# VectorE in emission order in the projection part of a Conformer layer, with new estimates in the emission's planner

## The chip, the cores and the metric

The kernel runs on one core of a Trainium2 chip. The metric is device time in microseconds (us) of one execution, as the median of several runs. PE is TensorE's matmul row in the profile, PEld its weight loads, DVE is VectorE, ACT ScalarE, POOL GpSimd, and SP the queue that issues most transfers.

## The reference, cut to what matters

One layer of a streaming encoder is computed in float32 for a prompt of 2048 frames and a sample of 64 frames with cached keys, values and convolution rows. D is 1024.

```python
h = rms_norm(x, norm1_g) * (1 + sc1) + sh1          # modulation: silu(c) @ w_ada + b_ada
glu_a, glu_b, q, k, v, g_conv, g_attn = split(h @ w_in)
u = glu_a * sigmoid(glu_b)
y = silu(layer_norm(causal_depthwise_conv(u, w_dw, 31 taps) + b_dw)); conv_out = y @ w_conv_out
q, k = rms_norm per head (8 heads of 64)
p = softmax(q k^T / 8 + rel_bias[clipped distance], own chunk of 64 and 8 chunks before)
attn_out = (p v) @ w_attn_out
x = x + gt1 * ((sigmoid(g_conv) * conv_out + sigmoid(g_attn) * attn_out) @ w_o)
h2 = rms_norm(x, norm2_g) * (1 + sc2) + sh2
x = x + gt2 * ((silu(gate) * up) @ w_ffn_out)       # gate, up = split(h2 @ w_ffn_in)
```

Outputs are the new rows of prompt and sample, and the states of convolution, keys and values.

## The kernel before, in words

**Precision.** A float32 operand is split into a high part, rounded by an ACT copy, and a low part, the DVE or POOL difference (`split`, L681). A product is three matmuls: high by high, high by low, low by high (`mm3`, L675). So nearly every result on its way to the next product passes ACT, then DVE.

**Two parts.** The first, the projection part, goes over four token blocks of 576 or 512 tokens (`PBLOCKS`). In each block the stages come in the order q, 0, k, 1, v, 2, 3, g (`ORDER`): the projections q, k and v (`qkv`, L1100); four stages 0 to 3 of the gated convolution input, 128 channels each (`glu`, L1141); and the two gates g (`gates`, L1244). Beside those matmuls run the attention heads of the block before or of the same block (`attend`, L1380), the convolution (`convolve`, L1167), its layer norm (`conv_norm`, L1186), and the norm and transposes of the next block's tokens (`norm_tile`, L1076). Attention goes over eight heads per block, and in block 0 eight heads of the sample besides: 40 heads. The second part merges the branches and does the output projection and the feed-forward layer over three token blocks. In the profile it begins at about 1222 us.

**Work on DVE in the projection part.** A convolution stage is 31 instructions per 128 channels over 512 or 606 columns, the taps: one `tensor_scalar`, then 30 `scalar_tensor_tensor` into tile y. They need nothing but u and the tap before. Beside them stand short links in chains of other engines: per score tile, the mask-and-maximum (`softmax_max`, L1279: tile pr, with the maximum in sm), then an exponential on ACT, then a reciprocal and a scaling on DVE (`softmax_scale`, L1294); the low halves pl of the transposed weights; the norms of q and k (kn, ssq); the low halves part_l of what is stored (`store_kq` L950, `conv_norm`, `finish_head` L1322), whose high halves part_h come from ACT. part_h and part_l have two buffers each (NS, L732), which a store to device memory empties. DVE also copies results out of PSUM (u, vst, h) and splits weights at their first use (wlo).

**What sets the order.** The Python code emits instructions in one sequence and keeps a planner beside it. `Meter` (L84) wraps each engine; every emission passes `Stream.add` (L176), which adds an estimated duration to that engine's estimated clock (`load`). L101, the line of the wrapper, is therefore the line of nearly all instructions in the profile, and they are told apart by tiles. PE's estimated clock is the planner's "now". Every 500 estimated ns (STEP_NS) a tick calls the lanes (`Lane`, L106): norm_lane, work, attn, tail and conv. A lane lets its next generator emit a step when the step's due time has come and the engines' estimated backlogs over PE are under the lane's room: 2000 ns of DVE for conv (CONV_ROOM), up to four taps per tick; 3000 ns of DVE and 4000 ns of ACT for attn. A step names when it may go on, as the estimated end of an engine's work (`when`, L197) plus a lag: PE_LAG is 400 ns, DMA_LAG, the allowance for a transfer, 4000 ns. `softmax_max` is called directly behind the score matmuls, in the same step; the taps come from the conv lane in later pumps. At the start of a block's stage 0, `conv.drain()` (L1540) emits what is left of the taps.

The order on the chip is not yet that of emission. When the program is built, the framework's scheduler puts each engine's instructions in order by its own model: among those that its model holds ready, it takes the one emitted first. An instruction whose inputs it holds not ready is passed by later ones. Semaphores follow from that order. Each engine then works through its list.

Of the kernel before, what the change touches and what calls it, by code (L numbers as in the profile page):

```python
# [63 lines left out]
def token_tiles(lo, hi):  # L64
    head = [(0, SMP)] if lo == 0 else []
    return head + [(t, P) for t in range(max(lo, SMP), hi, P)]
# [39 lines left out]
class Lane:  # L106
# [7 lines left out]
    def add(self, gen):  # L114
        self.gens.append([gen, 0.0, {}])
# [52 lines left out]
class Stream:  # L168
# [7 lines left out]
    def add(self, name, op, n, args, kw):  # L176
        if name == "pe":
            x = args[1]
            if op == "transpose":
                ns = 128 / 1.2  # L180
            elif x.dtype == F32:
                ns = max(n, 64) / (2.4 if "tile_position" in kw else 0.6)
            else:
                ns = (n if n >= 256 else 512) / 2.4
        elif name == "act":
            ns = 220 + 0.83 * n
        elif name == "pool":
            ns = 260.0 * n if ALU.pow in args else 60 + 2.25 * n
        else:
            fast = op in ("tensor_scalar", "tensor_copy")  # L190
            ns = 75 + n * (8.3 if op == "reciprocal" else 0.75 if fast else 1.04)
        self.load[name] = max(self.load[name], self.load["pe"]) + ns

    def full(self, room):
# [392 lines left out]
def streaming_layer(ctx: ExitStack, tc: tile.TileContext, I, O):  # L587
# [87 lines left out]
    def mm3(ps, lh, ll, rh, rl, first, last, **kw):  # L675
        pe.matmul(ps, lh, rh, start=first, stop=False, **kw)
        pe.matmul(ps, lh, rl, start=False, stop=False, **kw)
        pe.matmul(ps, ll, rh, start=False, stop=last, **kw)
        stream.spend()

    def split(hi, lo, src):  # L681
        act.activation(hi, src, AF.Copy)
        stream.after("dve", "act")
        dve.tensor_tensor(lo, src, hi.bitcast(F32), ALU.subtract)
# [49 lines left out]
    def temp(name, shape=(P, 512)):  # L734
        return wk.tile(list(shape), F32, tag="t", name=name, bufs=NT)
# [62 lines left out]
    def mod_sums(pa, keys):  # L798


        for i, key in enumerate(keys):
            w = M.get(key)
            a, b = w.shape[1:]
            for j in range(4):

                k, c = divmod(j * 2 * P, b)
                pe.matmul(
                    pa[32 * j : 32 * j + 32], cl[:, a * i + k], w[:, k, c : c + 2 * P], start=i == 0,
                    stop=i == len(keys) - 1, tile_position=(0, 32 * j),
                )  # L810
            M.done()

    def mod_rows(pa):
        R = temp("R", pa.shape)
        stream.after("dve", "pe")
        dve.tensor_copy(R, pa)
        return R

    def mod_columns(pc, R, c6, ct, nh):


        pc = pc.rearrange("p (e n) -> p e n", e=2)
        for e in range(2):
            pe.matmul(pc[:, e], R[:, e * P : e * P + P], sel, start=True, stop=True)
        stream.after("dve", "pe")
        pc = pc[:, :, 2 * (nh - 1) : 2 * (2 * nh - 1)].rearrange("p e (h s) -> p e h s", h=nh)
        cs = slice(ct, ct + 2 * nh)

        def place(a):
            return a[:, cs].rearrange("p (h e) s -> p e h s", e=2)  # L830

        def wide(a):
            return a.rearrange("p (h e) -> p e h", e=2).unsqueeze(3).to_broadcast([P, 2, nh, 2])

        bias = wide(b_ada[:, 8 * c6 + ct : 8 * c6 + ct + 2 * nh])
        gates_of = lambda i: gates_c[:, i].rearrange("p s k -> p k s")
        out = place({0: B1, 1: A1, 3: B2, 4: A2}[c6] if c6 not in (2, 5) else gates_of((2, 5).index(c6)))
        dve.tensor_tensor(out, pc, bias, ALU.add)
        if c6 in (1, 4):
            dve.tensor_tensor(out, out, wide({1: g1, 4: g2}[c6][:, cs]), ALU.mult)  # L840
        elif c6 in (2, 5):
            dve.tensor_scalar(out, out, {2: 0.25, 5: 0.5}[c6], None, ALU.mult)
# [22 lines left out]
    def first_block(xs):  # L865

        tiles = token_tiles(*PBLOCKS[0])
        vectors, taps = setup()
        taps = taps()
        for x_t, (t, n) in zip(xs, tiles):  # L870
            r = square(x_t, n)
            dve.tensor_scalar(x_t[:n], x_t[:n], r, None, ALU.mult)

        def modulation(ct):

            pa = ps_a.tile([P, 512], F32, tag="o", name="pa")
            cs = [slice(c6 * 2 * P, (c6 + 1) * 2 * P) for c6 in range(2)]
            for c6, c in enumerate(cs):
                mod_sums(pa[:, c], [("mod", c6, ct // 2, h, 0) for h in range(2)])
            R = mod_rows(pa)  # L880

            def rest():
                for c6, c in enumerate(cs):
                    mod_columns(pa[:, c], R[:, c], c6, ct, 1)

            return rest

        def turn(k):
            pt = ps_a.tile([P, 2, 512], F32, tag="s", name="pt")
            for i, (t, n) in enumerate(tiles):  # L890
                o = pt[:, 0, t : t + n] if i < 4 else pt[:, 1, :n]
                pe.transpose(o, xs[i][:n, k * P : (k + 1) * P], ident[:n, :n])
            h = wk.tile([P, QB + SMP], F32, tag="pr", name="h32", bufs=8)
            for a, e, o, w in ((0, SMP, pt[:, 0, :SMP], 1), (SMP, 448, pt[:, 0, SMP:448], 0), (448, 576, pt[:, 1, :P], 0)):
                dve.tensor_scalar(h[:, a:e], o, A1[:, k, w : w + 1], B1[:, k, w : w + 1], ALU.mult, ALU.add)
            split(hh[:, k], hl[:, k], h)

        rest = modulation(0)
        vectors()
        rest()  # L900
        W.open("", "wst")
        turn(0)
        pss = [ps_g.tile([P, 512], F32, tag="gp", name="ps") for _ in tiles]
        ws = {}

        def product(i, k):
            t, n = tiles[i]
            if k // 2 not in ws:
                ws[k // 2] = W.get(("qkv", 0, k // 2))
            wh, wl = ws[k // 2]  # L910
            mm3(pss[i][:n], hh[:, k, t : t + n], hl[:, k, t : t + n], wh[:, k % 2], wl[:, k % 2], k == 0, k == KT - 1)
            if i == len(tiles) - 1 and k % 2:
                W.done()

        for k in range(KT - 2):
            if k == 2:
                next(taps)
            turn(k + 1)
            if k and k % 2 == 0:
                rest = modulation(k + 2)  # L920
            for i in range(len(tiles)):
                if i == 2 and not k:
                    rest = modulation(k + 2)
                if i == (2 if k else 4) and k % 2 == 0:
                    rest()
                product(i, k)
        turn(KT - 1)
        for i, (t, n) in enumerate(tiles):
            for k in (KT - 2, KT - 1):
                product(i, k)  # L930
            work.start(qk_rows(pss[i], n, gqk[:, 0:1], q_d, t, None, i > 2))
        next(taps, None)
# [82 lines left out]
    def cached_kv():  # L1015
        rows_ = [(src, j) for j in range(CACHE // P) for src in (ck, cv)]
        ts = []
        for i, (src, j) in enumerate(rows_):
            for src_, j_ in rows_[len(ts) : i + 2]:
                t = temp("cache")  # L1020
                nc.sync.dma_start(t, src_[j_ * P : (j_ + 1) * P])
                ts.append((t, stream.load["pe"] + CACHE_LAG))
            t, landed = ts[i]
            yield landed
            if src is ck:
                store_kq(t, P, k_d, j * P)
            else:
                store_v(t, P, j * P)
            yield
# [38 lines left out]
    def square(x_t, n):  # L1068
        ssq = wk.tile([P, 2], F32, tag="ssq", name="ssq", bufs=3)
        for j in range(2):  # L1070
            act.activation(temp("junk")[:n], x_t[:n, 512 * j : 512 * j + 512], AF.Square, accum_out=ssq[:n, j : j + 1])
        stream.after("dve", "act")
        dve.tensor_tensor(ssq[:n, 0:1], ssq[:n, 0:1], ssq[:n, 1:2], ALU.add)
        return rsqrt_mean(wk, ssq[:n, 0:1], n, 1, D)
# [418 lines left out]
    M.fill()  # L1493
    W = Weights((nc.sync, act, dve, gps), wpool, dram, stream, list(weight_order()), source, 3, 5, lambda key: key[0] in KEPT)
    first_block(xs)
    norm_lane.add(cached_kv())
    mods = mod_steps()
    norms = {}
# [55 lines left out]
    conv.drain()  # L1554
    tail.drain()
    stream.flush()
    side.close()
    p1.close()

# [524 lines left out]
```

## Time and profile before

| what | us |
|---|---|
| median of 3 runs | 3047.5 |
| lowest, highest | 3043.02, 3049.83 |
| the profiled execution, its own time | 3036.07 |
| its span, first to last instruction | 3034.3 |
| busy in the span: PE | 2931.0 |
| DVE | 1928.2 |
| ACT | 1263.8 |
| POOL | 1204.7 |

The profiled execution's time is 1.77 us more than its span. Rows of a timeline give the start, the duration, engine, line, operation, out<-in tiles and shapes, and in brackets the engine's idle time before it with what ended it. Rows of waits give who waited for whom: total us, times, longest us. Rows of groups give busy us, mean ns of one, and idle us before. Rows of windows give the busy us of the engines PE, PEld, DVE, ACT and POOL, the granted PE clock as a share of full speed, the share of busy DMA engines, and GB/s. Rows of transfers end in the KB of one and the median us from issue to landing.

### The profile page before, as it was taken

The page shows a single profiled execution, that of the slowest core. Times are in us where ns is not written, and L with a number is a line of the kernel's source. Part 1 is how long each engine was busy: PE and PEld are TensorE (multiplying, and loading weights), DVE is VectorE, ACT ScalarE, POOL GpSimd, SP SyncE. Part 2 cuts the span into 40 slices and gives each one's busy share as a digit, 9 for nine tenths or more (in the row PEclk, how much of TensorE's full clock was granted, in tenths as well). Part 3 has the DMA queues.
Part 4 walks back from the last instruction along what each step waited for, and adds up shares of the span by engine and source line. Part 5 has one row for each costly group of instructions (what it writes and reads, how often), then busy time and mean ns, then how long its engine had stood idle before and what let it go on. Part 6 is the DMA issues. An engine that isn't in the chain of part 4 may idle for free.

```text
span 3034.3 us, 44863 instructions
## 1 busy us (share of the span) xinstructions
PE 2931.0 (97%) x16277; PEld 2603.6 (86%) x16277; DVE 1928.2 (64%) x3668; ACT 1263.8 (42%) x2290; POOL 1204.7 (40%) x785
## 2 busy tenths in 40 slices
PE   7999898999999999989999989999999999999999
PEld 4789776887888788878999889899999998999998
DVE  4897687777977895464444535555665655366565
ACT  2334532452255257464444324534444254344441
POOL 0201110111011102378888633347766343367761
PEclk9999999999999999999999999999999999999999
DMA  9788789888997788886444686433334965333334
GB/s 314 269 297 302 232 290 303 265 266 272 292 294 232 257 264 264 261 284 215 150 143 145 230 298 211 160 115 111 115 94 143 335 220 191 111 95 114 118 92 162
DMA packets 472107, 646.93 MB, mean 213 GB/s; under 512 B 36820, under 2 KB 315208, under 8 KB 471885
## 3 DMA queue, kind: packets, MB, share of 16 engines
q1 hardware_dynamic: 459605, 626.68, 63.1%
q10 hardware_dynamic: 12280, 17.39, 1.6%
q8 instruction: 128, 2.10, 0.3%
q14 instruction: 94, 0.77, 0.1%
HBM read 487.02 MB, written 156.93 MB: 212 GB/s over the span
## 4 chain that ended last, share of the span: by engine, by line
PE 80%; DVE 9%; DMA 4%; ACT 2%; POOL 2%; issue 2%; SPq 1%; ACTq 0%; POOLq 0%; DVEq 0%
PE ps L101 51%; PE pd L101 16%; PE pw L101 6%; DVE y L101 4%; PE po L101 2%; PE sc L101 2%; PE ptp L101 2%; POOL wlo L101 1%; PE pt L101 1%; DVE pr L101 1%; PE pa L101 1%; ACT whi L101 1%; DVE wlo L101 1%; DMA x_t<-in_x_prompt 1%; POOL ws L101 0%
## 5 line engine op out<-in xcount | busy, mean ns | idle before, releaser
L101 POOL TENSOR_TENSOR wlo<-wst,whi 128x1024 fp32r<-128x1024 f32 (+1 forms) x215 | 456.6, 2133 | 343.1 <-ACT whi L101 320.9
L101 PE MATMUL ps<-t,whi 128*128 128x384 f32 (+1 forms) x2112 | 501.8, 322 | 7.2 <-DVE v L101 4.4
L101 ACT ACTIVATE whi<-wst 128x1024 fp32r<-128x1024 f32 (+1 forms) x270 | 261.6, 973 | 339.1 <-PE ps L101 120.7
L101 PE MATMUL ps<-b,whi 128*128 128x384 f32 (+1 forms) x1584 | 380.1, 326 | 8.8 <-ACT early L101 8.4
L101 PEld LDWEIGHTS ps<-t,whi 128*128 128x128 f32 x2112 | 367.8, 188 | 12.9 <-DVE v L101 3.4
L101 DVE SCALAR_TENSOR_TENSOR y<-u,wd,y 128x512 f32<-128x512 f32 (+1 forms) x480 | 369.1, 772 | 6.6
L101 PE MATMUL ps<-hh,whi 128*128 128x512 f32 (+2 forms) x992 | 361.9, 365 | 0.2 <-DVE part_l L101 0.2
L101 PE MATMUL ps<-hh,wlo 128*128 128x512 f32 (+2 forms) x992 | 345.4, 348 | 1.2 <-DMA wlo<-w_din_l 1.2
L101 PE MATMUL ps<-hl,whi 128*128 128x512 f32 (+2 forms) x992 | 345.3, 348 | 0.0
L101 PE MATMUL ps<-t,wlo 128*128 128x384 f32 (+1 forms) x1056 | 339.5, 322 | 4.0 <-POOL wlo L101 4.0
L101 PE MATMUL pd<-whi,hid 128*128 128x512 f32 (+1 forms) x1076 | 342.1, 390 | 1.1 <-ACT hid L101 1.1
L101 DVE TENSOR_TENSOR acc<-acc,pd 128x512 f32<-128x512 f32 (+1 forms) x398 | 269.8, 686 | 95.5 <-PE pd L101 93.4
L101 PEld LDWEIGHTS ps<-b,whi 128*128 128x128 f32 x1584 | 277.9, 189 | 14.5 <-ACT early L101 10.4
L101 PE MATMUL ps<-b,wlo 128*128 128x384 f32 (+1 forms) x792 | 256.3, 324 | 0.0
L101 POOL TENSOR_TENSOR r<-t,mhalf 128x8 f32<-128x8 f32 (+3 forms) x68 | 83.2, 1226 | 392.7 <-DVE t L101 377.7
L101 PEld LDWEIGHTS pd<-whi,hid 128*128 128x128 f32 (+1 forms) x1076 | 197.2, 183 | 47.3 <-ACT hid L101 1.5
L101 POOL TENSOR_TENSOR wlo<-ws,whi 128x512 fp32r<-128x512 f32 x144 | 190.3, 1336 | 80.2 <-ACT whi L101 78.4
L101 POOL TENSOR_TENSOR wlo<-wup,whi 128x1024 fp32r<-128x1024 f32 (+1 forms) x70 | 150.7, 2154 | 150.5 <-ACT whi L101 98.5
L101 PE MATMUL pd<-wlo,hid 128*128 128x512 f32 (+1 forms) x538 | 210.0, 390 | 0.0
L101 PEld LDWEIGHTS ps<-hh,wlo 128*128 128x128 f32 x992 | 187.1, 189 | 23.8 <-DMA wlo<-w_din_l 1.6
L101 PEld LDWEIGHTS ps<-hh,whi 128*128 128x128 f32 x992 | 187.6, 189 | 18.6 <-issue 2.1
L101 PEld LDWEIGHTS ps<-t,wlo 128*128 128x128 f32 x1056 | 198.5, 188 | 5.2 <-POOL wlo L101 4.6
(222 smaller groups left out, 6017.3 us busy)
## 6 DMA issues: line engine op xcount, KB each, us to landing
whi<-w_din_h SPq DMA_DIRECT2D x72, 512.0 KB, 6.1
wlo<-w_din_l SPq DMA_DIRECT2D x72, 512.0 KB, 6.8
wst<-sum_d SPq DMA_DIRECT2D x132, 256.0 KB, 3.0
wfo<-in_w_ffn_out SPq DMA_DIRECT2D x49, 512.0 KB, 5.5
wmod<-in_w_ada SPq DMA_DIRECT2D x48, 512.0 KB, 7.0
sum_d<-ws SPq DMA_DIRECT2D x88, 256.0 KB, 2.0
wst<-in_w_ffn_in SPq DMA_DIRECT2D x84, 256.0 KB, 3.2
wst<-in_w_ffn_in SPq DMA_DIRECT2D x37, 512.0 KB, 5.5
```

The costliest lines, as they stand in the source:

```text
L101: return f(*args, **kw)
```

## The change

Three lines of the planner and a region. In `Stream.add`, a float32r matmul is estimated 13.5 ns longer; a DVE instruction has a fixed part of 240 ns when it is a `scalar_tensor_tensor` (the taps among them) and 110 ns otherwise, where it had 75 ns. These estimates serve the whole kernel. And from behind `first_block` to behind the flush that ends the projection part, a region tells the framework's scheduler to keep DVE's instructions in the order of emission. The other engines, and the transfers' issue order, stay with the scheduler.

```diff
             else:
-                ns = (n if n >= 256 else 512) / 2.4
+                ns = 13.5 + (n if n >= 256 else 512) / 2.4
...
             fast = op in ("tensor_scalar", "tensor_copy")
-            ns = 75 + n * (8.3 if op == "reciprocal" else 0.75 if fast else 1.04)
+            ns = (240 if op == "scalar_tensor_tensor" else 110) + n * (8.3 if op == "reciprocal" else 0.75 if fast else 1.04)
...
     first_block(xs)
+    in_order = tc.manual_schedule(engines={mybir.EngineType.DVE})
+    in_order.__enter__()
     norm_lane.add(cached_kv())
...
     stream.flush()
+    in_order.__exit__(None, None, None)
     side.close()
```

## The prediction

> **What bounds the kernel now.** The page comes first: its span, and the share of the matrix engine PE.
>
> ```profile
> span 3034.3 us, 44863 instructions
> PE 2931.0 (97%) x16277; PEld 2603.6 (86%) x16277; DVE 1928.2 (64%) x3668; ACT 1263.8 (42%) x2290; POOL 1204.7 (40%) x785
> ```
>
> PE is the bound: 103 us of the span are left without it. Next, the table by stage: the projection part's crowded first block, its other blocks, and the rest (columns: PE, PEld, DVE, ACT, POOL busy, clock, DMA share, GB/s).
>
> ```profile
> 100.00:500.00 400.00, 370.41 (x2220) 321.00 (x2219) 318.38 (x662) 149.14 (x325) 49.85 (x51) 0.96 0.83 277
> 500.00:1222.00 722.00, 709.17 (x3846) 594.84 (x3845) 570.31 (x1183) 324.43 (x599) 89.05 (x74) 1.00 0.84 270
> 1222.00:3034.30 1812.30, 1773.23 (x9754) 1634.37 (x9752) 987.31 (x1704) 757.46 (x1308) 1051.61 (x637) 0.99 0.52 171
> ```
>
> In the region of the new order PE lacks 29.6 us in the first 400 and 12.8 us in the next 722, so 42 us are all that an order on DVE could win in idle time. DVE, the VectorE, is busy 80% and 79% there: not the bound, but without much slack. Next, PE's waits in that part (us in total, times, longest).
>
> ```profile
> PE ptp L101 <- DVE pr L101: 14.9, 10, 8.9
> PE sc L101 <- DVE sm L101: 4.4, 7, 1.3
> PE ps L101 <- ACT hh L101: 3.6, 2, 2.9
> PE ps L101 <- DMA whi<-w_dqkv_h: 3.2, 1, 3.2
> ```
>
> The two largest entries are the softmax of the attention heads, made by DVE. One of those waits is the largest stall, 8.9 us; so the timeline around it, DVE first and PE behind.
>
> ```profile
> 463.96 0.75 DVE L101 SCALAR_TENSOR_TENSOR y<-u,wd,y 128x512 f32<-128x512 f32 x1
> ...
> 470.36 4.68 DVE L101 SCALAR_TENSOR_TENSOR y<-u,wd,y 128x512 f32<-128x512 f32 x6
> 474.96 0.48 DVE L101 CUSTOM_DVE_ANT_0 pr<-sc,bias 64x320 f32<-64x320 f32 x1
> ...
> 477.62 0.37 DVE L101 TENSOR_SCALAR pr<-pr,sm 64x320 f32<-64x320 f32 x1
> ```
>
> ```profile
> 468.83 0.46 PE L101 MATMUL sc<-kk,q 128*64 128x320 f32 x2
> 478.14 0.55 PE L101 MATMUL ptp<-ident,pr 64*128 64x64 f32 x3 [8.86 <-DVE pr L101]
> ```
>
> The scores are there at 469.3, yet DVE first works through six convolution taps (y) and takes the scores at 474.96. Nothing else fed PE: it stood until 478.14. By the code softmax_max is emitted straight behind its score matmuls, and the taps that a later tick hands out come behind it. This is the pattern that emission order forbids. It recurs on a smaller scale, around 198 us and at 508 us:
>
> ```profile
> 195.70 2.61 DVE L101 SCALAR_TENSOR_TENSOR y<-u,wd,y 128x606 f32<-128x606 f32 x3
> 198.23 0.28 DVE L101 CUSTOM_DVE_ANT_0 pr<-sc,bias 128x128 f32<-128x128 f32 x1
> ```
>
> ```profile
> 196.02 0.34 PE L101 MATMUL sc<-kk,q 128*128 128x128 f32 x2
> 198.57 0.50 PE L101 MATMUL sc<-kk,q 128*128 128x256 f32 x2 [0.56 <-DVE sm L101]
> 199.74 0.61 PE L101 MATMUL sc<-kk,q 128*128 128x384 f32 x2 [0.67 <-DVE sm L101]
> 201.10 0.79 PE L101 MATMUL sc<-kk,q 128*128 128x512 f32 x2 [0.75 <-DVE sm L101]
> ```
>
> ```profile
> 508.37 0.85 PE L101 MATMUL sc<-kk,q 128*128 128x320 f32 x4 [1.34 <-DVE sm L101]
> ```
>
> **The change, part by part.** The first part, *order*: it removes no work, and adds none. Where it helps, the taps ahead of a softmax go behind it. The stalls shown sum to 8.86 + 0.56 + 0.67 + 0.75 + 1.34 = 12.2 us. I count them as gone; what is late next is the rest of the same softmax chain, on ACT, and projection matmuls run beside that. The clock follows the stalls:
>
> ```profile
> 200.00:210.00 10.00, 8.15 (x38) 7.11 (x38) 8.43 (x23) 4.09 (x10) 0.00 (x0) 0.66 0.99 363
> 480.00:490.00 10.00, 10.00 (x44) 8.25 (x43) 1.14 (x3) 1.07 (x3) 0.00 (x0) 0.92 0.74 239
> ```
>
> In the ten microseconds from 200 a third of the clock was withheld, in those from 480 a twelfth: (1 - 0.66) x 8.15 + (1 - 0.92) x 10.0 = 3.6 us of matmul time. Removal so far: 12.2 + 3.6 = 15.8 us. [...]
>
> Second, *estimates*. A tap of 512 columns was put at 75 + 1.04 x 512 = 607 ns and is now put at 240 + 532 = 772; a matmul of 512 columns goes from 213 to 227, one of 384 from 160 to 173.5.
>
> ```profile
> L101 DVE SCALAR_TENSOR_TENSOR y<-u,wd,y 128x512 f32<-128x512 f32 x360 | 268.3, 748 | 4.7
> ...
> L101 DVE SCALAR_TENSOR_TENSOR y<-u,wd,y 128x512 f32<-128x512 f32 (+1 forms) x480 | 369.1, 772 | 6.6
> ...
> 1954.44 16.36 PE pd L101 x72
> 1970.81 20.82 PE ps L101 x120
> ```
>
> The trace has 748 ns for the tap (six start 0.78 us apart at 470.36), 16.36 / 72 = 227 ns for 512 columns and 20.82 / 120 = 173.5 ns for 384. So the new figures are right, and the old ones let the emission believe that the 480 taps cost about 480 x 0.165 = 79 us less than they do. With an order that is obeyed this matters: a lane hands out taps only while DVE's estimated backlog is under 2.0 us (CONV_ROOM), and PE's consumers are put 0.4 us (PE_LAG) behind DVE's estimated end. I expect the backlog ahead of a softmax to shrink from the six taps above to two or three. I give this no gain of its own; without it the order's gain would not hold.
>
> Third, *what the order costs*. The new wait is at the head of DVE's queue: an instruction that is not ready holds all that stands behind it, the taps and also the copies that free PSUM. Two kinds stand out. The low halves (part_l) wait for ACT's high halves, which wait until a store has emptied one of two buffers; the store's landing is in no estimate. ACT's waits, from 100 to 500 us and then from 500 to 1222:
>
> ```profile
> ACT part_h L101 <- DMA q_d<-part_h: 8.3, 2, 6.0
> ACT part_h L101 <- DMA c_d<-part_h: 3.9, 2, 2.3
> ```
>
> ```profile
> ACT part_h L101 <- DMA k_d<-part_h: 16.2, 2, 8.6
> ACT part_h L101 <- DMA c_d<-part_h: 3.9, 1, 3.9
> ```
>
> ```profile
> DVE part_l L101 <- ACT part_h L101: 9.9, 11, 2.9
> DVE pr L101 <- PE sc L101: 29.6, 31, 3.3
> ```
>
> That is 32.3 us in seven waits, of which DVE shows only 9.9 today, because taps slip past. At 198 us DVE was 198.23 - 196.36 = 1.9 us late and PE lost 0.56, so PE has a lead of about 1.3 to 2 us; I take 2. The seven waits were 6.0, 2.3, 2.3, 1.6, 8.6, 7.6 and 3.9 us, the longest given, its partner the remainder; less 2 each they are 4.0 + 0.3 + 0.3 + 0 + 6.6 + 5.6 + 1.9 = 18.7 us. That is the upper end; the lower end is nothing, because the scheduler still orders PE and can put other matmuls there. I take 4: the 6.0 us wait, in the block where DVE is busy 80% and PE already stalls. Later PE lacks only 12.8 us of 722, though the waits for k_d lie there too, and has projection matmuls to go on with; I cost those at nothing. If that cover is gone, the other waits cost 14.7.
>
> The other kind is the softmax of a new head, whose matmuls wait for loads. The planner counts 4.0 us for a landing; the issues say 5.4 and 5.0:
>
> ```profile
> q<-q_d SPq DMA_DIRECT2D x64, 256.0 KB, 5.4
> kk<-k_d SPq DMA_DIRECT2D x48, 256.0 KB, 5.0
> ```
>
> So DVE may stand 1.4 us at each of 40 heads (8 in each of four blocks, and 8 of the sample), 56 us in all. It has 400 - 318 + 722 - 570 = 234 us idle to put that in, and 1.4 is under PE's lead: nothing for PE. If the lead is only the planned 0.4 us, they cost PE 40 x 1.0 = 40 us.
>
> Fourth, *after 1222 us* only the estimates act. No time of an instruction changes, PE lacks 39 us of 1812, and events tied to PE's estimated clock come 6 to 8% earlier, counted in matmuls. I take nothing, with 6 us to either side.
>
> **Sum.** -15.8 + 4 = about -12 us. The profiled execution took 3036.07 us, 1.8 around its span; it would take 3024. The median of the three timed runs is 3047.5, 0.4% above the profiled one. The prediction is for such a median: 3047.5 - 12 = 3035.5 us.
>
> **The rivals.**
>
> *The queue's head decides* (slower). The same order that stops taps from slipping past also stops them where nothing was lost. Place: part_l and the first softmax of a head. Price: the whole 18.7 us, with the gain cancelled because the late scores at 468.83 now hold DVE from 463.96 on and all later softmaxes shift. 3047.5 + 18.7 = 3066; with the 40 us of the heads, 3106. It decides once a hold exceeds PE's lead of 2 us. For it: seven such waits, and a DVE busy 80%. Against: the largest of these waits lie where PE today loses least. [...]
>
> *More than the named stalls goes.* The two DVE rows of PE's waits are 14.9 + 4.4 = 19.3 us, and the clock of 0.96 in the first stage withholds 0.04 x 370 = 14.8; with 4 us of holds that is -30, or 3017. Against: some of these waits have other causes than taps, and the clock also follows waits for DMA.
>
> *Taps come too late.* Taps at 772 ns fill the 2.0 us sooner, so fewer are handed out per tick and the rest is emitted in one run where a block drains its convolution. Ten taps left in each of three blocks would hold DVE 10 x 0.78 = 7.8 us, less 2 of lead: 17 us, 3065. Against: 80% busy leaves room for all of them.
>
> *It does not change the time.* The scheduler reorders PE, ACT and the DMA queues around the new DVE order, and other stalls replace these: 3047.5, give or take 6.
>
> **How the numbers follow.** A measurement of this kernel can tell about 0.2%, 6 us, from no change. Forecast (6 to 22 us faster) 0.32; more than that 0.12; no change 0.14; the queue's head 0.30; late taps 0.12. So faster 0.44, same 0.14, slower 0.42. The forecast's own range is 3025 to 3041. Both signs hold much of the chance, so the range for 8 in 10 goes from 3010, past the large gain, to 3085, half of the heads' 40 us on top of 3066.
>
> **What would show it.** Right: no run of taps between the end of a score matmul and its softmax; PE's wait for pr under 5 us in total; PE busy above 375 of 400 us in the first stage; clock above 0.96 there. Wrong: DVE's idle time rises above 300 us, with part_l and pr waiting longest, and PE waits for copies out of PSUM (u, vst, kn), or PE lacks more than 45 us after 1222.

## The result, and the profile after

The changed kernel takes 3087.05 us (median of 4 runs, 3085.94 to 3088.94), the kernel before, run beside it, 3046.13 us (median of 4, 3043.02 to 3049.83): a ratio of 1.0143, 95% interval 1.0126 to 1.0161. It is **slower** by 41 us. The prediction said 3035.5, and its range ended at 3085. The profiled execution of the changed kernel took 3085.94 us.

The page of the changed kernel: its span, the busy time of the engines, and the chain of work that ended last by engine.

```profile
span 3084.1 us, 44919 instructions
...
PE 2954.7 (96%) x16277; PEld 2611.6 (85%) x16277; DVE 1945.5 (63%) x3668; ACT 1262.5 (41%) x2290; POOL 1208.0 (39%) x785
...
PE 73%; DVE 10%; DMA 9%; ACT 3%; issue 2%; POOL 2%; SPq 1%; ACTq 0%; DVEq 0%; POOLq 0%
```

The work is the same (16277 matmuls, 3668 DVE instructions), but transfers are 9% of the chain, against 4% on the page of before. The stages, as they were shown of before:

```profile
100.00:500.00 400.00, 370.08 (x2213) 318.85 (x2215) 323.32 (x665) 149.23 (x325) 51.72 (x49) 0.97 0.84 276
500.00:1222.00 722.00, 692.28 (x3654) 567.84 (x3642) 560.46 (x1135) 288.97 (x546) 72.02 (x68) 0.98 0.80 259
1222.00:3084.10 1862.10, 1816.28 (x9957) 1672.02 (x9957) 1013.90 (x1758) 791.04 (x1362) 1070.52 (x647) 0.99 0.52 171
```

The first 400 us hold 2213 matmuls where they held 2220: nothing won, nothing lost. The next 722 us hold 3654 instead of 3846. At 709.17 / 3846 = 0.184 us each, those 192 missing matmuls are 35 us. That is where most of the time goes. The first matmul of the next stage (tile cin) shows the whole loss of the projection part; of before, then of after, shortest, median and longest ns, and first and last start:

```profile
L101 PE MATMUL ps<-cin,whi x768: 277/334/687, 1219.9 to 2500.1; 128*128 128x384 f32 x128, 128*128 128x320 f32 x32, 128*128 128x256 f32 x32
```

```profile
L101 PE MATMUL ps<-cin,whi x768: 274/334/657, 1264.4 to 2548.3; 128*128 128x384 f32 x128, 128*128 128x320 f32 x32, 128*128 128x256 f32 x32
```

It starts 44.5 us later; the spans differ by 49.8, so some 5 us more are lost behind it, and nearly all of the loss is inside the region of the new order. Next, what VectorE waits for from 100 to 1260 us (total us, times, longest), before and then after:

```profile
DVE pr L101 <- PE sc L101: 30.9, 32, 3.3
DVE part_l L101 <- ACT part_h L101: 10.9, 13, 2.9
DVE pr L101 <- DMA bias<-rb_d: 2.2, 3, 1.1
```

```profile
DVE pr L101 <- PE sc L101: 93.1, 35, 9.6
DVE pr L101 <- DMA bias<-rb_d: 30.5, 6, 7.1
...
DVE part_l L101 <- ACT part_h L101: 16.4, 13, 4.8
```

The two waits of a softmax (pr), for its scores and for its bias, went from 33.1 to 123.6 us; part_l hardly moved. One such wait, close up: VectorE, then PE, then SP's issues, and the ten microseconds from 1160.

```profile
1157.26 0.75 DVE L101 SCALAR_TENSOR_TENSOR y<-u,wd,y 128x512 f32<-128x512 f32 x1
1163.60 0.82 DVE L101 CUSTOM_DVE_ANT_0 pr<-sc,bias 128x640 f32<-128x640 f32 x1 [5.59 <-DMA bias<-rb_d]
```

```profile
1151.86 0.74 PE L101 MATMUL sc<-kk,q 128*128 128x320 f32 x4
...
1159.73 0.50 PE L101 MATMUL po<-ph,vv 128*128 128x512 f32 x1
1162.19 0.82 PE L101 MATMUL sc<-kk,q 128*128 128x320 f32 x4 [1.96 <-DMA kk<-k_d]
1164.49 1.43 PE L101 MATMUL sc<-kk,q 128*128 128x320 f32 x4 [1.48 <-DVE sm L101]
```

```profile
1152.63 0.60 SPq L1308 DMA_DIRECT2D q<-q_d  x1
...
1155.32 1.94 SPq L1352 DMA_DIRECT2D bias<-rb_d  x2
```

```profile
1160.00:1170.00 10.00, 5.75 (x18) 4.41 (x18) 6.30 (x14) 3.28 (x7) 0.00 (x0) 0.66 0.41 111
```

The new head's first transfer is issued at 1152.63; the last of its six is issued until 1157.26, and VectorE gets the bias at 1163.6, about 11 us after the first issue. The planner counts 4.0 us for this. The loads could not be issued sooner: by the code q and kk have one buffer each (`load_qk`, bufs=1), and the last scores that read them ended at 1151.86 + 0.74 = 1152.60. VectorE's next instruction in emission order is that softmax, so it stands for 5.59 us and the taps stay behind it. PE ends its other work, waits 1.96 us for kk and 1.48 for the softmax, and a third of its clock is withheld: in these ten microseconds it is busy 5.75 us. The clock in the trace is half from 1163.16 to 1169.98. A stretch ahead of that, then its two halves:

```profile
1159.75:1163.16 3.41, 1.30 (x7) 0.75 (x5) 0.00 (x0) 0.91 (x2) 0.00 (x0) 1.00 1.02 242
1163.16:1166.57 3.41, 1.43 (x4) 1.03 (x4) 2.90 (x6) 0.93 (x2) 0.00 (x0) 0.50 0.25 97
1166.57:1169.98 3.41, 3.25 (x9) 2.77 (x10) 3.38 (x8) 1.68 (x3) 0.00 (x0) 0.50 0.00 0
```

In the first of them PE was busy 1.30 us at the full clock; in the next two the clock was half, also in the last, where PE was busy 3.25 us. In the stretch ahead of the half clock PE's longest gap was 1.96 us, and PE was busy 38% of it.

PE's waits for kk itself, from 100 us to the end of that part, before and then after:

```profile
PE sc L101 <- DMA kk<-k_d: 1.8, 2, 1.2
```

```profile
PE sc L101 <- DMA kk<-k_d: 10.2, 9, 2.0
```

So the late loads reach PE by two ways: through VectorE, and at the head of PE's own queue.

### The profile page after: what moved, and what is told of

Its sections match the earlier page's. It is cut to its first block, busy times and chain, and to the rows that moved or that the text cites. A ratio compares the mean times of both kernels' runs of the same rounds, so it can differ in the third digit from the quotient of the medians.

```text
span 3084.1 us, 44919 instructions
## 1 busy us (share of the span) xinstructions
PE 2954.7 (96%) x16277; PEld 2611.6 (85%) x16277; DVE 1945.5 (63%) x3668; ACT 1262.5 (41%) x2290; POOL 1208.0 (39%) x785
## 4 chain that ended last, share of the span: by engine, by line
PE 73%; DVE 10%; DMA 9%; ACT 3%; issue 2%; POOL 2%; SPq 1%; ACTq 0%; DVEq 0%; POOLq 0%
PE ps L101 45%; PE pd L101 15%; PE pw L101 6%; DVE y L101 5%; PE sc L101 2%; PE po L101 2%; DMA kk<-k_d 2%; PE ptp L101 1%; DVE pr L101 1%; DMA bias<-rb_d 1%; POOL wlo L101 1%; PE pt L101 1%; DVE pl L101 1%; DVE wlo L101 1%; PE pa L101 1%
## 5 line engine op out<-in xcount | busy, mean ns | idle before, releaser
L101 DVE TENSOR_TENSOR acc<-acc,pd 128x512 f32<-128x512 f32 (+1 forms) x398 | 269.9, 686 | 95.3 <-PE pd L101 93.3
L101 PEld LDWEIGHTS pd<-whi,hid 128*128 128x128 f32 (+1 forms) x1076 | 197.2, 183 | 45.8
L101 PEld LDWEIGHTS ps<-hh,whi 128*128 128x128 f32 x992 | 188.2, 190 | 23.8 <-ACT gate L101 4.3
L101 PE MATMUL ps<-cin,whi 128*128 128x384 f32 (+2 forms) x768 | 188.6, 332 | 16.4 <-DVE t L101 9.9
```

Of the source, the lines that this page charges most:

```text
L101: return f(*args, **kw)
```

## The experiments

Theory **H**: in emission order a head's first softmax stands at VectorE's queue head until q, kk and bias have landed, and the allowance of 4.0 us in `fetch` puts it there too early. Rival **T**: the new estimates hand out taps or attention too late. Rival **P**: part_l behind the stores. Each run is compared with runs of the kernel before on the same chip (medians 3040.4 to 3043.3 in four groups), by ratio.

**The order alone.** The region, with the old estimates.

```diff
+    in_order = tc.manual_schedule(engines={mybir.EngineType.DVE})
+    in_order.__enter__()
...
+    in_order.__exit__(None, None, None)
```

> The region of emission order, with the old estimates. Theory H (the head of VectorE's queue stands for a new head's loads, whose landing the planner puts at 4.0 us): the order alone is the cause, so at least as slow as the change, 3075 to 3110 us, with VectorE's waits for sc and bias near 120 us. Rival T (the new estimates make taps and attention late): the order alone is near the kernel before, 3040 to 3055.

3088.53 us, ratio 1.015 [1.0134, 1.0166]: the whole loss. Its VectorE waits from 100 to 1260 are 93.3 us for scores and bias, under the 120 foretold, and 44.1 for part_l:

```profile
DVE pr L101 <- PE sc L101: 83.0, 45, 12.9
DVE part_l L101 <- ACT part_h L101: 44.1, 18, 6.5
DVE pr L101 <- DMA bias<-rb_d: 10.3, 3, 5.4
```

**The estimates alone.** The two lines of `Stream.add`, without the region.

> The new estimates without the region. Theory H: within 10 us of the kernel before, 3036 to 3056 us. Rival T: most of the loss is here, 3070 to 3090, with VectorE's waits for sc and bias near the 32 us of before.

3046.62 us, ratio 1.0017 [1.0007, 1.0027]: T falls as the cause of the 41 us. The estimates cost at most 0.3% by themselves.

**A longer allowance.** The change, with 8.0 us in `fetch` only.

```diff
-            loaded[i] = stream.load["pe"] + DMA_LAG
+            loaded[i] = stream.load["pe"] + HEAD_LAG   # 8000.0
```

> The change, with the planner's allowance for the loads of a new head raised from 4.0 to 8.0 us (that one place, other allowances as they were). Theory H: VectorE's waits for sc and bias fall from 124 us to under 60, and the time to 3045 to 3065 us. Rival T and rival P (part_l behind the stores that empty its two buffers): 3080 to 3095, since neither is touched.

3036.71 us, ratio 0.9982 [0.9971, 0.9992]: one number takes back the 41 us and a little more. The time is below the 3045 to 3065 expected. Its waits (every line is one further down in this kernel):

```profile
DVE pr L102 <- PE sc L102: 40.6, 33, 4.1
DVE part_l L102 <- ACT part_h L102: 27.6, 18, 4.3
DVE pr L102 <- DMA bias<-rb_d: 5.8, 3, 3.5
```

The pr waits fall to 46.4 us, while part_l's are larger than in the change (27.6 against 16.4). So P is not what decides.

**The bias loaded once.** The change, where only the first head loads its bias and all others use it.

```diff
-            if now["bias"] is None or now["bias"][0] != h:
+            if now["bias"] is None:
```

> The change, with the bias loaded for the first head alone; the other heads use that head's bias, so 7 of 8 bias loads per block are left out. Theory H: the wait of pr for bias (30 us) goes, and part of the wait for sc, since loads of q and k come sooner: 3055 to 3075 us. Rivals T and P: within 8 us of the change, 3079 to 3095.

3075.65 us, ratio 1.0109 [1.0093, 1.0124]: a gain of 10 to 11 us over the change, 0.65 us above the 3055 to 3075 expected. The wait for the bias shrinks to 5.4 us, but the wait for the scores grows to 114.5 where it was to fall: with the last two of the six transfers gone, VectorE waits for the scores instead. The edit leaves out more than the expectation says: the trace has 2 issues for the bias in place of 64, one load for the whole kernel.

**Six and ten microseconds.** As above, with 6000.0 and with 10000.0.

> The change with the allowance for a head's loads at 6.0 us. Theory H (it is the size of this allowance that decides under emission order): between the change (3087) and the run with 8.0 (3037), about 3055 to 3065 us, with the waits of pr for sc and bias between the two. If any perturbation of the emission had the same effect, there is no order between 4, 6, 8 and 10.

3031.00 us, ratio 0.9957 [0.994, 0.9973], against 3055 to 3065 expected: a miss. Less allowance was needed than H had said.

> The change with the allowance at 10.0 us. Theory H: the waits of pr are gone already, so no more is gained there; 40 heads that start 2 us later each lengthen the attention that is left after the last projection matmul (30 us with 8.0) by 10 to 16 us: 3040 to 3055 us.

3032.01 us, ratio 0.9966 [0.9954, 0.9979], against 3040 to 3055: a miss in the other direction, since a longer allowance cost nothing.

**The allowance without the order.** The kernel before, with 8.0 us.

> The kernel before (no region, old estimates) with the allowance at 8.0 us. Theory H: there the scheduler lets other work pass a softmax that waits, so the allowance buys nothing: 3040 to 3060 us. If the allowance is a gain of its own, it is near 3000 to 3030.

3050.78 us, ratio 1.003 [1.002, 1.0041]: without the order the longer allowance does not help.

**Order and allowance, old estimates.** The region and 8.0 us.

> The region with the old estimates and the allowance at 8.0 us. If the new estimates of taps and matmuls carry weight under emission order, this is 10 to 30 us slower than the run with all three (3037): 3047 to 3067. If only the order and the allowance matter: 3031 to 3043.

3062.86 us, ratio 1.0071 [1.0055, 1.0087]: 26 us above the run with the new estimates (3036.71). Under an order that is obeyed the estimates are worth that much, once the loads' stand does not cover it.

**Five, three, and three without the order.**

> The change, with the allowance for a new head's loads at 5.0 us in place of 4.0 (6.0 gave 3031, 4.0 gave 3087). H (VectorE's queue stands for loads that land after the allowance; the issues show medians of 5.0 to 5.8 us): about half of the loads are still late, so the time lies between, 3045 to 3070, and VectorE's waits of pr for sc and for bias in the projection part between 65 and 124 us. If a cause other than the landing time were met by chance at 6.0, the times would not be ordered by the allowance: 5.0 as slow as 4.0, or slower.

3046.93 us, ratio 1.0012 [1.0, 1.0024], with 88.8 us of pr waits: within the expectation, and the times from 4.0 to 6.0 are ordered by the allowance.

> The change, with the allowance at 3.0 us. H: each new head's softmax is put 1 us further ahead of its loads than in the change: 32 heads of the projection part by up to 1 us, slower than 3087: 3095 to 3120, with more than 124 us of waits of pr for sc and bias. If the wait is not for the loads, no worse than 3087.

3086.16 us, ratio 1.014 [1.0121, 1.0158]: a miss. The pr waits grew to 137.3 us, but the time stayed that of 4.0. The waits for the bias (30.5 us with 4.0) tell of the earlier place, though the time does not rise with it:

```profile
DVE pr L102 <- PE sc L102: 77.3, 40, 7.6
DVE pr L102 <- DMA bias<-rb_d: 60.0, 11, 8.3
```

> The kernel before, with the allowance at 3.0 us and no emission order. H: taps slip past a softmax whose loads are late, so the allowance hardly matters here: 3035 to 3055, within 0.4% of the kernel before. If it is as much slower as 3.0 is under the order, the order is not what makes the allowance matter.

3050.36 us, ratio 1.0027 [1.0014, 1.004]: without the order, 3.0 and 8.0 cost the same 0.3%.

**Nothing to land.** Since 3.0 was no worse than 4.0, it was open whether the loads cost, or the place among the taps. This kernel leaves out the loads of q, kk and bias in all but the first head of blocks 1 to 3 (the other heads compute with the first head's data); the allowance stays at 4.0. Run on the change and on the kernel before:

```diff
-            now["qk", i] = load_qk(h, *spans(x))
-            if now["bias"] is None or now["bias"][0] != h:
+            again = h > 0 and x in (1, 2, 3)
+            now["qk", i] = now["qk", i - 1] if again else load_qk(h, *spans(x))
+            if not again and (now["bias"] is None or now["bias"][0] != h):
```

> The change, its allowance left at 4.0 us, with the loads of q, kk and bias left out for all but the first head of blocks 1 to 3 (the other 21 heads use the first head's tiles; same instructions otherwise, other data). H (the order costs because the loads land later than 4.0 us): with nothing to land, 21 of the 24 holds of these blocks go, and blocks 1 to 3 lose nothing: 3025 to 3050, with VectorE's waits of pr for sc and for bias together under 60 us. Rival (an allowance of 4.0 us puts the softmax at a bad place among the taps, whatever the loads do): 3070 to 3090.

> The kernel before with the same loads left out: what the loads cost without the order, and the measure for the run above. H: taps slip past late loads here, so little goes: 3020 to 3045, and the order on top of it (the run above) within 15 us of it. Rival: 30 us or more between the two.

With the order 3053.67 us, ratio 1.0035 [1.0022, 1.0048]; without it 3034.67, ratio 0.9974 [0.9963, 0.9985]. By the ratios, leaving the loads out is worth 33 us under the order and 8 without it, and the order's price falls from 41 us to 19 (3053.67 - 3034.67). The first is 4 us above H's 3025 to 3050 and 16 under the rival's 3070 to 3090; the 19 lie between H's 15 and the rival's 30. The pr waits of the first are 65.8 us, not under 60:

```profile
DVE pr L101 <- PE sc L101: 57.4, 32, 9.0
...
DVE pr L101 <- DMA bias<-rb_d: 8.4, 2, 5.3
```

Most of them lie in block 0, where the loads stay. From 500 to 1260 us they are 35.0, where the change has 93.6 and the kernel before 23.8:

```profile
DVE pr L101 <- PE sc L101: 35.0, 25, 9.0
```

Part of the 19 us is block 0, too. The two kernels up to 435 us and from there to 1200, with the order and then without:

```profile
100.00:435.00 335.00, 309.78 (x1881) 273.13 (x1879) 266.03 (x543) 131.64 (x282) 46.30 (x45) 0.97 0.83 271
435.00:1200.00 765.00, 746.55 (x4037) 620.99 (x4036) 624.56 (x1269) 317.15 (x606) 79.96 (x74) 0.99 0.69 237
```

```profile
100.00:435.00 335.00, 314.67 (x1930) 277.66 (x1928) 277.54 (x577) 137.14 (x295) 48.09 (x47) 0.98 0.83 274
435.00:1200.00 765.00, 748.11 (x4053) 627.13 (x4054) 600.16 (x1254) 326.40 (x616) 85.46 (x76) 0.99 0.70 237
```

Up to 435 us, 49 matmuls fewer, at 314.67 / 1930 = 0.163 us, are 8 of the 19. From 435 to 1200 it is 16 fewer, at 748.11 / 4053 = 0.185 us 3 of the 19; with the loads, the change has 142 fewer there than the kernel before (3886 against 4028), 26 us. So in that stretch the late loads make nearly all of the order's price. What makes the last 8 of the 19 us wasn't shown.

The sum of VectorE's waits alone does not give the time. With 6.0 us the pr waits are 65.4 us (46.8 + 18.6) at 3031.00, here 65.8 at 3053.67; the order alone has 93.3 at 3088.53, the allowance of 5.0 us 88.8 at 3046.93.

**A version that beats both.** With 8.0 or 10.0 us the projection matmuls end earlier than before, and the last block's attention is left over behind them. So the change, with 10.0 us in blocks 0 to 2 and 6.0 in block 3; and the same allowances on the kernel before.

```diff
-            loaded[i] = stream.load["pe"] + DMA_LAG
+            loaded[i] = stream.load["pe"] + HEAD_LAG.get(x, 10000.0)   # {3: 6000.0}
```

> The change, with an allowance of 10.0 us in the heads of blocks 0 to 2 and of 6.0 us in block 3. H: the first three blocks end as with 10.0 throughout (the projection matmuls some 37 us before those of the kernel before), and less of the last block's attention is left behind the last projection matmul than the 38 us of 10.0: 3015 to 3030, the fastest version. If the tail of attention is set by its own loads and not by the allowance, 3028 to 3036, as 6.0 or 10.0 throughout.

3020.42 us, ratio 0.9919 [0.9902, 0.9937]: the fastest version, by 0.8%. Its last projection matmul starts at 1176.2, the next stage at 1206.1, and what lies between:

```profile
L102 PE MATMUL ps<-hl,whi x992: 274/389/504, 79.4 to 1176.2; 128*128 128x512 f32 x109, 128*128 128x288 f32 x77, 128*128 128x256 f32 x13
```

```profile
L102 PE MATMUL ps<-cin,whi x768: 278/334/656, 1206.1 to 2485.3; 128*128 128x384 f32 x128, 128*128 128x320 f32 x32, 128*128 128x256 f32 x32
```

```profile
1176.50:1206.10 29.60, 21.09 (x92) 16.96 (x90) 14.81 (x37) 18.81 (x34) 2.91 (x2) 0.71 0.36 100
```

Before, that last matmul started at 1214.6. Of the 38 us won there, 30 - 5 = 25 go into a tail of attention in which PE is busy 21.09 of 29.6 us at a clock of 0.71, with no projection matmuls left to fill it. With 10.0 us throughout the tail is 38 us, and most of the gain is gone.

> The kernel before with the allowance of the fastest version (10.0 us in blocks 0 to 2, 6.0 in block 3), without the order and with the old estimates. H: the allowance pays only under the order: 3035 to 3055, within 0.4% of the kernel before. If the allowance by block helps by itself: 3015 to 3030, and the order has no share in the fastest version.

3044.47 us, ratio 1.0003 [0.9994, 1.0013]: by itself the allowance does nothing. The fastest version needs the order.

## Why the prediction was wrong, point by point

**What bounds the kernel: right.** PE is the bound before and after, and 42 us of idle in the region were all there was to win; the best version's gain (22 us) is about half of that.

**What the order removes: right at one place, wrong as a rule.** The six taps ahead of the softmax at 470 us are gone. The same place after the change, VectorE and then PE:

```profile
465.53 0.49 DVE L101 TENSOR_SCALAR pr<-pr,sm 128x512 f32<-128x512 f32 x1
473.95 0.48 DVE L101 CUSTOM_DVE_ANT_0 pr<-sc,bias 64x320 f32<-64x320 f32 x1 [7.93 <-PE sc L101]
```

```profile
473.46 0.46 PE L101 MATMUL sc<-kk,q 128*64 128x320 f32 x2
473.75 0.40 PE L101 MATMUL ps<-whi,hl 128*128 128x512 f32 x1
476.73 0.52 PE L101 MATMUL po<-pl,vv 128*128 128x512 f32 x1 [2.58 <-DVE pl L101]
```

VectorE now stands idle for 7.93 us in front of that softmax, and PE's wait is 2.58 us instead of 8.86. But in the first 400 us PE is busy 370.08 us where it was busy 370.41: what was won at the named stalls was lost at others, and the 15.8 us of the first term did not appear as a sum. Nor does the order keep taps from standing in front of a ready softmax. PE is not held to the order of emission, so score matmuls can run ahead of taps that were emitted before them. PE, then VectorE:

```profile
552.61 0.84 PE L101 MATMUL sc<-kk,q 128*128 128x320 f32 x4
```

```profile
559.36 6.26 DVE L101 SCALAR_TENSOR_TENSOR y<-u,wd,y 128x512 f32<-128x512 f32 x8
...
566.37 0.82 DVE L101 CUSTOM_DVE_ANT_0 pr<-sc,bias 128x640 f32<-128x640 f32 x1
```

These scores were done at 553.45 and taken at 566.37, behind twelve taps. The same happens at 595.81, 849.41 and 878.95, with eleven or twelve taps. "This is the pattern that emission order forbids" was wrong: six taps were the most ahead of a ready softmax before.

**What the order costs: the step that failed.** The prediction wrote of the heads' loads: "So DVE may stand 1.4 us at each of 40 heads ... and 1.4 is under PE's lead: nothing for PE." Two things in it were wrong. The 1.4 us was the median landing of one transfer less the allowance. A head has six transfers, and the issues alone take SP 3.8 us; one head of the changed kernel:

```profile
823.50 0.61 SPq L1308 DMA_DIRECT2D q<-q_d  x1
...
826.15 1.18 SPq L1352 DMA_DIRECT2D bias<-rb_d  x2
```

The last issue begins at 826.15 + 0.59 = 826.74, 3.2 us after the first, and a bias takes 5.8 us from issue to landing:

```profile
bias<-rb_d SPq DMA_DIRECT2D x64, 144.0 KB, 5.8
```

Together that is an estimate of 9.0 us, 5.0 above the allowance, where the prediction had 1.4. The six waits of a softmax for its bias were 5.1 us on average (30.5 / 6). The other mistake was that PE's lead covers it: holds of 5 us are above the 2 us of lead that the prediction itself had read off. Its rival *The queue's head decides* had the mechanism. That its 40 us for the heads are nearly the measured 41 is luck: they were 40 holds of 1.4 us over a lead of 0.4 us, and the range took in only half of them. Part_l, to which it gave its first 18.7 us, was the smaller part. The term that was put at nothing measures 25 of the 41 us by the runs without the loads of 21 heads (33 under the order, less 8 without it); the forecast had -15.8 + 4 = -12 in all.

How it reached PE: from 100 us to the next stage PE had 40.7 us idle before (1114.80 - 1074.07, to the last projection matmul) and 61.7 after (1159.40 - 1097.69).

```profile
100.00:1214.80 1114.80, 1074.07 (x6030) 910.99 (x6029) 885.05 (x1838) 469.56 (x918) 136.53 (x124) 0.98 0.84 272
```

```profile
100.00:1259.40 1159.40, 1097.69 (x6044) 915.98 (x6043) 902.79 (x1843) 465.88 (x915) 138.22 (x125) 0.98 0.80 261
```

So 21.0 of the 44.6 us between these two ends are idle time, and 23.6 are time in which PE counts as busy: 1097.69 / 6044 = 181.6 ns a matmul against 178.1. By an estimate the clock accounts for a part of that: four score matmuls of 320 columns took 0.74 us at 1151.86, at the full clock, and 1.43 at 1164.49, at half of it, and over windows of ten microseconds (1 - clock) x busy time sums to 11 us before and 18 after, 7 us more. What makes the other 16 or so wasn't shown. The prediction priced holds in idle time alone.

**The estimates: half right.** "I give this no gain of its own" stands beside 26 us under the order with a fitting allowance, and beside nothing in the change itself (3088.53 without them, 3087.05 with them). *Taps come too late* fell.

**After 1222 us: right.** About 5 us more were lost behind the projection part, within the 6 that were left to either side. The sign of PE lacking more than 45 us after 1222 was just met (1862.10 - 1816.28 = 45.8), but in the changed kernel that row takes in the end of the projection part.

**The signs.** Of the four signs of being right, one came, a clock above 0.96 in the first stage (0.97). Runs of taps in front of a ready softmax were still there (above), PE was busy 370.08 us and not above 375, and its wait for pr fell only from 14.9 to 10.2 us where it was to be under 5:

```profile
PE ptp L101 <- DVE pr L101: 10.2, 11, 2.5
```

VectorE's idle time in the region did not pass 300 us (400 - 323.32 + 722 - 560.46 = 238): it stood more in front of softmaxes and less elsewhere. The sum of its idle time was the wrong sign to watch; the row of one wait told where to look, though not how much PE would lose.

**What stays open.** Why 3.0 us is no slower than 4.0; what makes the 8 us that neither block 0 nor the stretch to 1200 us accounts for without loads; what makes the 16 us of busy time that the clock does not; and how much of the wait for scores is the landing itself and how much the place that the scheduler gives the score matmuls in PE's queue. At 473.46 the scores ran without a wait of their own, behind projection matmuls, so there it was PE's order. Taken wait by wait, about 62 of the 93.1 us of the change end at scores that PE ran without a wait, where it was about 28 of 30.9 before; about 25 end at scores for which PE had itself waited for kk. More buffers for q, kk, the bias or the parts weren't tried.

## What to carry to other kernels

Before an engine is put in program order, look at each instruction that will stand at its queue's head, and compare the time the planner allows its inputs with the time from the first issue of the whole group of transfers to the landing of the last, not with the median of one. That comparison shows where to look and not the best number: 6.0 us were enough here, with a group that takes an estimated 9.0. An order and the planner's numbers are one change: here the order cost 1.4% with an allowance of 4.0 us and won 0.2 to 0.8% with 6.0 to 10.0, while without the order none of the allowances that were run helped. Keeping one engine in order does not keep its work next to another engine's, as that one may still run ahead. Where work ends earlier, look at what is left behind it: most of what the better allowance won went into a tail of attention with no matmuls beside it.

## What the runs showed of the hardware

An issue of a head's loads held SP's queue for about 0.6 us (823.50 to 827.33 for six), and at 1155.32 two for the bias held it for 1.94, so at these two heads the last load was issued some 3 us or more after the first. In the changed kernel the granted clock was 0.50 from 1163.16 to 1169.98; in the 3.41 us ahead of that it was 1.00, and PE was busy 1.30 us, with gaps of at most 1.96 us. In the kernel before it was 0.50 from 201.63 to 208.45; in the 3.41 us ahead of that it was 1.00, and PE was busy 1.64 us, with gaps of at most 0.75 us.
